# Norm passes of caches and late weights issued only in the units of branch A

## The chip, the cores and the metric

The kernel runs on one core of a Trainium2 chip. The metric is the device time of one launch in microseconds (us). The core has five engines with a queue each: TensorE (PE, with its weight loads as PEld), VectorE (DVE), ScalarE (ACT), GpSimd (POOL) and SyncE (SP). In this kernel SP issues every DMA, so that all loads, stores and DMA transposes stand in one queue, in the order in which the program was built.

## What is computed

The reference is one layer of a streaming encoder: 2048 prompt rows and 128 sample rows (8 streams of 16) of width 1024. Cut to what matters here:

```
h  = rms_norm(x, norm_g) * (1 + scale) + shift          # scale, shift, gate from c @ w_ada + b_ada
qa, ka, va, za, qb, kb, vb, zb, ga, gb = split(h @ w_in)
A: 4 heads, two score maps each, chunk-causal:  w = softmax(s1) - lam * softmax(s2);  oa = w @ va
B: 8 heads, stick-breaking:  a = sigmoid(z) * prod over later keys of (1 - sigmoid(z));  ob = a @ vb
ya = (rms_norm(oa) * silu(za)) @ w_branch_a;   yb = (ob * silu(zb)) @ w_branch_b
y  = rms_norm(x + gate * ((sigmoid(ga) * ya + sigmoid(gb) * yb) @ w_out), final_g)
```

The sample rows attend to caches of 512 earlier keys and values (cache_a_k, cache_a_v, cache_b_k, cache_b_v) as well. All rotated keys and values are outputs too.

## The kernel before

**Numbers.** Products of f32 operands are made of two f16 halves each, three matmuls for one. To split an operand, the kernel needs a bound on its size: the sum of its squares. For the weights and caches that are used late (w_branch_a, w_branch_b, w_out and the four caches) these sums come from 80 *norm passes*, here called spares: `norms()` at L801 makes a list of them. Each takes the next of a ring of staging buffers (`free`), loads 128 x 1024 f32 into it (512 KB, SP, L811) and squares and sums it on ACT (L255). Nothing reads their sums before `early_work` (L1153) and the last stage.

**Stages.** First (L875 to L1084) the conditioning, the norms and the transposed f16 halves of h, which go to DRAM (hT_d). Then the attention loop (L1171 to L1198), and last the output stage with the sample rows' attention (L1203 on).

**Units.** The attention loop goes over 8 units u and in each over 17 tiles: the sample tile NT, and the row tiles t = 0 to 15. Even units are one head of branch A, odd units two heads of branch B; below they are called A0, B1, A2, B3, A4, B5, A6, B7. In each step the loop issues scores of tile t (L597; matmuls L611, L612), the product with the values for the tile two steps back (L663 for B, L659 to L661 for A), and projections for a tile some five steps ahead (L409; gate columns L476). The work of a tile grows with t, since the attention is causal.

**What each engine does.** In an A tile DVE evicts the scores (L530), ACT takes exponentials (L119), DVE combines the two maps (L575) and splits them with ACT. In a B tile ACT takes two sigmoids (L119), DVE runs the product as a scan (L588), POOL multiplies (L594), ACT casts (L544) and DVE subtracts (L545). In both, SP then issues a DMA transpose of the weights (wt, L552) for PE. SP also loads h for the projections (hg, L386, three buffers), and stores keys, values and z (L457 to L460), gates (L480) and outputs (L653).

**Preparing weights.** When a unit starts, `prepare_unit` (L290) puts the pieces for the next unit's projection weights into the list `back`: loads into ring buffers (L305, and L307 for the gate columns), their Squares, and cuts into f16 halves (L273, L275, L278), in which DVE, ACT and POOL read the loaded buffer. The loop issues one or two of these in each step until `back` is empty, which it is from tile 9 on in units 0 to 6. In unit 7 nothing is prepared. When a unit's projection starts, five tiles before its scores, the buffers of the unit before it return to the ring. Before that the ring holds few buffers: 6 in A0, 4 in the middle units, 2 in A6, because the last unit's gate weights are twice as wide.

**Where spares are issued.** In a step with an empty `back` the loop issues spares: the length of the list, divided by a count of steps that are left, rounded up.

**Order.** The order in which Python issues the work is only a priority. The framework's scheduler decides the order on each engine: it lifts an instruction ahead of others once its buffers are free, loads on SP above all. The order is then fixed in the program.

**After the spares.** `early_work` starts when the projections and the spares are all issued.

Of the kernel before, what the change touches and what calls it, by code (L numbers as in the profile page):

```python
# [32 lines left out]
NT = SEQ // P  # L33
# [57 lines left out]
def interleave(*streams):  # L91

    order = []
    for i, pieces in enumerate(streams):
        lo, hi = 0.0, 1.0
        if isinstance(pieces, tuple):
            pieces, lo, hi = pieces
        total = sum(cost for cost, _ in pieces) or 1.0  # L100
        done = 0.0
        for j, (cost, fn) in enumerate(pieces):
            order.append((lo + (hi - lo) * (done + cost / 2) / total, i, j, fn))
            done += cost
    for _, _, _, fn in sorted(order, key=lambda e: e[:3]):
        fn()
# [3 lines left out]
def layer_kernel(ctx: ExitStack, tc: tile.TileContext, a: dict):  # L110
# [486 lines left out]
    def scores(U, t, jobs):  # L597

        sc, kind = U["sc"], U["kind"]
        nch = t // 4 + 1  # L600
        own = [new_job(U, t, c, t + 1) for c in range(1 + kind)]
        jobs += own

        def chunk(c, ch):
            job = own[c if kind == 1 else 0]
            seg = job["segs"][ch * 4 // SEG]
            n = 512 if ch < t // 4 else (t % 4 + 1) * P
            p = bank("s")
            qst, kk = U["q", t], U["k"][ch]
            diag = ch == t // 4  # L610
            T.matmul(p[:, 0:n], qst[:, c, :], kk[:, c, 0:n], start=True, stop=False)  # L611
            T.matmul(p[:, 0:n], qst[:, 2 + c, :], kk[:, c, 0:n], start=False, stop=not diag)  # L612
            if diag:
                m = mask_a if kind == 0 else mask_b
                T.matmul(p[:, n - m.shape[1] : n], idb, m, start=False, stop=True)
            evacuate(job, seg, c, p, ch * 512 - seg["lo"] * P, n, sc[:, 3:4], sc[:, 4:5], ch)
            if kind == 0:
                if diag and c == 1:
                    softmax_pair(job)
                return  # L620
            i = job["segs"].index(seg)
            later = job["segs"][i + 1] if i + 1 < len(job["segs"]) else None
            stick(seg, later, ch * 512 - seg["lo"] * P, n, p)
            if ch * 4 == seg["lo"]:
                if later is not None:
                    stick_weights(job, later, None)
                if i == 0:
                    stick_weights(job, seg, later)

        order = [(c, ch) for ch in range(nch) for c in range(2)] if kind == 0 else \  # L630
                [(c, ch) for c in range(2) for ch in reversed(range(nch))]
        return [(2.0 if ch < t // 4 else (t % 4 + 1) / 2, lambda c=c, ch=ch: chunk(c, ch)) for c, ch in order]
# [33 lines left out]
    def pv(job):  # L666

        U, t, c = job["U"], job["t"], job["c"]
        segs = job["segs"] if U["kind"] == 0 else job["segs"][::-1]
        order = [(seg, j) for seg in segs for j in range(seg["hi"] - seg["lo"])]  # L670

        def block(i):
            seg, j = order[i]
            if i == 0 and (U["kind"] == 0 or c == 0):
                U["po", t] = bank("o")
            pv_block(job, seg, U["po", t], j, U["v"][seg["lo"] + j], i == 0, i == len(order) - 1)
            if i == len(order) - 1 and (U["kind"] == 0 or c == 1):
                store(U, t, natural(U, t, U.pop(("po", t))))

        return [(1.5, lambda i=i: block(i)) for i in range(len(order))]  # L680
# [120 lines left out]
    def norms():  # L801

        srcs = [w[:, k, :] for w in (w_ba, w_bb) for k in range(4)] + [w_out[:, k, :] for k in range(KT)]
        srcs = [(src, wsums[:, i : i + 1]) for i, src in enumerate(srcs)]
        srcs += [(caches[name][:, i * 8 : i * 8 + 8, h * P : (h + 1) * P], csums[:, cache_column(name, h), i : i + 1])
                 for name in caches for h in range(4) for i in range(4)]

        def one(src, dst):
            st = free.pop(0)
            free.append(st)  # L810
            load(out=st if len(src.shape) == 2 else st.rearrange("p (j n) -> p j n", n=P), in_=src)  # L811
            sum_squares(st, 1024, dst)

        return [lambda src=src, dst=dst: one(src, dst) for src, dst in srcs]
# [3 lines left out]
    spare = norms()  # L818
# [36 lines left out]
    def position(x):  # L855

        m = min(int(x), len(steps) - 1)
        return starts[m] + (starts[m + 1] - starts[m]) * (x - m)

    def take(target, need):  # L860

        i = at[0]
        out = []
        while i < len(line) and (i < target or any(m <= need for m, _ in line[i : i + 14])):
            out.append((1.0, line[i][1]))
            i += 1
        at[0] = i
        return out

    def duration(t):  # L870
        return SAMPLE_TIME if t == NT else TILE_TIME + (t + 1) / 4
# [281 lines left out]
    def early_work():  # L1153


        res = ctx.enter_context(tc.tile_pool(name="resw", bufs=1, side="right", reuse_waits="tile"))
        L["wb"] = res.tile([P, 2, 2, 4, D], F16, name="wb")
        L["inp"] = ctx.enter_context(tc.tile_pool(name="inp", bufs=1, side="right", reuse_waits="tile"))
        L["s"] = [scales(total(add_up(wsums[:, lo : lo + 8], 8)), con, f"s_w{lo}") for lo in (0, 8)]
        stage = cutting.enter_context(tc.tile_pool(name="stage", bufs=1, side="right", reuse_waits="tile"))  # L1160

        def first(t):
            if "orms" not in L:
                L["orms"] = rsqrt(osums[:, 0:NT, :].rearrange("p t h -> p (t h)"), 4 * NT, P, con, "orms")
            states[t] = inputs(t)

        made = [lambda k=k, j=j, br=br: cut(L["wb"][:, br, :, :, :], (w_ba, w_bb)[br], k, j, L["s"][0], br + k, stage, "wst2", 1)
                for br in range(2) for k in (0, 2) for j in range(2)]
        return made + [lambda t=t: first(t) for t in tiles[0:2]]

    for n in range(len(steps) + PV_LAG):  # L1171
        made, qk, vs = [], [], []
        if n < len(steps):
            u, t = steps[n]
            past += duration(t)
            if t == NT and u < 7:
                back += prepare_unit(u + 1)
            if back:
                for fn in back[: -(-len(back) // max(1, W_READY - t % NT))]:
                    back.pop(0)()  # L1180
            else:
                for _ in spare[: -(-len(spare) // ((NT + 1 - t % NT) + 8 * (6 - min(u, 6))))]:
                    spare.pop(0)()
            if t < NT:
                qk = scores(units[u], t, made)
        if n >= PV_LAG:
            for job in jobs[n - PV_LAG]:
                vs += pv(job)
        target = position(len(steps) * past / whole + LEAD)
        pieces = take(target, min(n + 1, len(steps) - 1))  # L1190
        if at[0] == len(line) and not pieces and not spare:
            if cuts is None:
                proj.close()
                cuts = early_work()
            pieces = [(1.0, fn) for fn in cuts[: -(-len(cuts) // (len(steps) + PV_LAG - n))]]
            del cuts[: len(pieces)]
        interleave(pieces, qk, (vs, V_LO, V_HI))
        jobs.append(made)  # L1198
# [149 lines left out]
```

## Time and profile before

| | us |
|---|---|
| three runs | 2440.4, 2433.63, 2436.15 |
| their median | 2436.15 |
| the profiled execution | 2436.39 |
| its span (first to last instruction) | 2434.6 |

Mean granted clock of PE over the span: 0.949. In rows of the profile an instruction is named by its engine, its line in the kernel before, its operation and its tiles (out<-in), without buffer numbers: `wa` and `wb` are the ring's buffers. A wait row says who waited for whom, then us in all, the number of times and the longest. SPq is SP's queue. In a timeline row the first number is the start, the second the length, and what stands in brackets is the engine's idle time before it and what ended it.

### The profile page before, as it was taken

How to read it: one execution, taken by the hardware profiler on the slowest of the kernel's cores; microseconds unless marked ns; L12 is line 12 of the kernel's file. 1: busy time of each engine (PE TensorE's matmuls, PEld its weight loads, DVE VectorE, ACT ScalarE, POOL GpSimd, SP SyncE). 2: the span in 40 equal slices, each digit the busy share in tenths (PEclk: the TensorE clock that was granted, in tenths of full speed). 3: DMA queues.
4: the chain of work that ended last, by engine and by line, in shares of the span. 5: the costliest groups of instructions: out<-in, count | busy, mean ns of one | idle time of the engine just before them, and what ended most of it. 6: DMA issues, size and time to landing. Idle time of an engine off the chain costs nothing. (4 is left out here: it accounts for less than half of the span.)

```text
span 2434.6 us, 45193 instructions
## 1 busy us (share of the span) xinstructions
PE 2138.5 (88%) x16366; PEld 1252.6 (51%) x16366; DVE 1811.3 (74%) x3769; ACT 1601.5 (66%) x3200; POOL 840.5 (35%) x671
## 2 busy tenths in 40 slices
PE   4879998998999898899889889999974888989897
PEld 2445655565665455566555556555542344444443
DVE  4878787886667788667678975656787888887765
ACT  3758888886768887666778866656775544454552
POOL 1833033452202245310234631002354554445422
PEclk7979999999999999999999999999977889889999
DMA  9669869985876998577689756756679988888521
GB/s 328 218 207 228 195 158 233 216 177 136 208 198 158 222 196 179 133 169 184 158 191 194 161 139 166 158 126 138 142 168 239 276 226 238 221 232 225 163 101 53
DMA packets 854000, 453.98 MB, mean 186 GB/s; under 512 B 538922, under 2 KB 806362, under 8 KB 853264
## 3 DMA queue, kind: packets, MB, share of 16 engines
q1 hardware_dynamic: 853776, 451.09, 74.3%
q8 instruction: 128, 2.10, 0.4%
q14 instruction: 96, 0.79, 0.1%
HBM read 249.87 MB, written 73.44 MB: 133 GB/s over the span
## 5 line engine op out<-in xcount | busy, mean ns | idle before, releaser
L594 POOL TENSOR_TENSOR sc_p<-sc_p,sc_n 128x127 f32<-128x127 f32 (+7 forms) x192 | 320.0, 1669 | 765.4 <-DVE sc_n L588 734.4
L409 PEld LDWEIGHTS <-hg 128*128 128x128 f16 x3120 | 276.1, 99 | 312.4 <-DMA hg<-hT_d 61.0
L409 PE MATMUL ps_mm<-wa,hg 128*128 128x512 f16 x1590 | 400.3, 384 | 30.2 <-DMA hg<-hT_d 30.1
L409 PE MATMUL ps_mm<-wb,hg 128*128 128x512 f16 x1530 | 388.7, 383 | 19.1 <-DMA hg<-hT_d 19.1
L476 PEld LDWEIGHTS <-hg 128*128 128x128 f16 x2856 | 276.0, 98 | 92.8 <-DVE qst L504 4.3
L588 DVE TENSOR_TENSOR_SCAN sc_n<-ps_s,sc_n,zero_t 128x512 f32<-128x512 f32 x192 | 245.6, 1279 | 56.9 <-ACT ps_s L119 51.0
L611 PE MATMUL ps_s<-k,qst 128*128 128x512 f16 (+3 forms) x640 | 226.4, 355 | 36.3 <-DVE sc_n L588 32.2
L545 DVE TENSOR_TENSOR sc_n<-sc_p,sc_n 128x128 f16<-128x128 f32 (+7 forms) x192 | 227.7, 1191 | 27.7 <-ACT sc_n L544 27.3
L476 PE MATMUL ps_t<-wb,hg 128*128 128x256 f16 (+1 forms) x1734 | 244.5, 293 | 0.7 <-DVE qst L504 0.6
L119 ACT ACTIVATE sc_p<-ps_s,usc 128x512 f32<-128x512 f32 (+3 forms) x320 | 205.8, 643 | 46.5 <-PE ps_s L612 29.6
L612 PE MATMUL ps_s<-k,qst 128*128 128x512 f16 (+3 forms) x640 | 226.4, 355 | 0.0
L1235 PE MATMUL ps_mm<-wb,uT 128*128 128x512 f16 x816 | 199.8, 396 | 16.9 <-DVE o L1134 9.2
L119 ACT ACTIVATE ps_s<-ps_s,usc 128x512 f32<-128x512 f32 (+3 forms) x328 | 201.1, 613 | 0.0
L663 PE MATMUL ps_o<-v,wt 128*128 128x128 f16 x1088 | 161.2, 226 | 43.2 <-DMA wt<-sc_n 42.9
L1274 PE MATMUL ps_o<-wo,yT 128*128 128x512 f16 x816 | 193.4, 392 | 5.5 <-POOL wo L275 2.6
L442 POOL TENSOR_TENSOR rot<-pr,rope 128x256 f32<-128x256 f32 x68 | 61.9, 910 | 381.8 <-ACT pr L423 312.4
L544 ACT CAST sc_n<-sc_p 128x128 f16<-128x128 f32 (+7 forms) x192 | 155.1, 814 | 54.8 <-POOL sc_p L594 54.1
L530 DVE TENSOR_SCALAR_CACHE_REDUCE sc_p<-ps_s,usc 128x512 f32<-128x512 f32 (+3 forms) x160 | 106.6, 666 | 75.7 <-PE ps_s L612 54.8
L663 PEld LDWEIGHTS <-wt 128*128 128x128 f16 x1088 | 104.8, 102 | 98.3 <-DMA wt<-sc_n 54.1
L476 PE MATMUL ps_t<-wa,hg 128*128 128x256 f16 (+1 forms) x1122 | 148.4, 282 | 1.0 <-DVE qst L504 1.0
L664 PE MATMUL ps_o<-v,wt 128*128 128x64 f16 x1088 | 148.5, 198 | 0.0
L530 DVE TENSOR_SCALAR_CACHE_REDUCE sc_n<-ps_s,usc 128x512 f32<-128x512 f32 (+3 forms) x160 | 106.6, 666 | 48.9 <-PE ps_s L612 25.7
(317 smaller groups left out, 4566.0 us busy)
## 6 DMA issues: line engine op xcount, KB each, us to landing
hg<-hT_d SPq DMA_DIRECT2D x130, 512.0 KB, 4.6
g<-g_d SPq DMA_DIRECT2D x34, 512.0 KB, 7.1
out_dram<-pr SPq DMA_DIRECT2D x204, 64.0 KB, 1.9
g_d<-gt SPq DMA_DIRECT2D x102, 128.0 KB, 3.7
wide<-in_w_ada_dram SPq DMA_DIRECT2D x12, 1024.0 KB, 9.1
wa<-in_w_in_dram SPq DMA_DIRECT2D x34, 256.0 KB, 6.2
z_d<-pr SPq DMA_DIRECT2D x136, 64.0 KB, 1.8
o_d<-o SPq DMA_DIRECT2D x136, 64.0 KB, 2.9
```

What stands on the lines that cost most here:

```text
L119: i = S.activation(**kw)
L409: T.matmul(box["p"], box["h"][:, hi, k, :], U["w"][k][:, wi, :], start=(n == 0), stop=(n == 3 * KT - 1))
L476: T.matmul(box["g"][:, 0:gw], box["h"][:, hi, k, :], U["wg"][k // per][:, k % per, wi, :], start=(j == 0), stop=(j == 3 * KT - 1))
L530: V.tensor_scalar(out=dst[:, lo : lo + n], in0=p[:, 0:n], scalar1=sc_pos, scalar2=None, op0=ALU.mult, op1=ALU.max, accum_out=job["mx"][:, ...
L545: V.tensor_tensor(out=lo, in0=src, in1=hi, op=ALU.subtract)
L588: V.tensor_tensor_scan(out=dst[:, lo : lo + n][:, ::-1], data0=src[:, 0:n][:, ::-1], data1=zero_t[:, 0:1].to_broadcast([P, n]), initial=fi ...
L594: G.tensor_tensor(out=p[:, 0:m], in0=p[:, 0:m], in1=n[:, 1 : m + 1], op=ALU.mult)
L611: T.matmul(p[:, 0:n], qst[:, c, :], kk[:, c, 0:n], start=True, stop=False)
L612: T.matmul(p[:, 0:n], qst[:, 2 + c, :], kk[:, c, 0:n], start=False, stop=not diag)
L663: T.matmul(po[:, c * P : (c + 1) * P], wt[:, wj, :], vt[:, c, :, :], start=first, stop=False)
L1235: T.matmul(pb, st["u"][:, ui * 8 + br * 4 + k, :], wb[:, br, wi, k, c], start=(n == 0), stop=(n == 11))
L1274: T.matmul(po, st["y"][:, yi * 8 + k, :], wo[:, wi, k, c], start=(n == 0), stop=(n == 3 * KT - 1))
```

## The change

Spares are issued in even units alone (branch A), with another divisor: the steps left in this unit, plus four for each unit that is left before unit 6. In unit 6 the divisor is the number of tiles that are left, so that the list is empty after its last tile. The whole diff:

```diff
@@ -1178,8 +1178,9 @@
             if back:
                 for fn in back[: -(-len(back) // max(1, W_READY - t % NT))]:
                     back.pop(0)()
-            else:
-                for _ in spare[: -(-len(spare) // ((NT + 1 - t % NT) + 8 * (6 - min(u, 6))))]:
+            elif u % 2 == 0:
+
+                for _ in spare[: -(-len(spare) // ((NT - t % NT) + 4 * (6 - u)))]:
                     spare.pop(0)()
             if t < NT:
                 qk = scores(units[u], t, made)
```

`-(-a // b)` is a / b rounded up; W_READY is 9 and NT is 16. The list of spares and their order in it stay as they are, so that another spare falls on a given step, and the ring hands its buffers to other loads from there on.

## The prediction

> **What bounds the kernel now.** I read the page first, then busy time by unit (stretches), then PE's and SP's waits, then the timelines of two stalls.
>
> ```profile
> span 2434.6 us, 45193 instructions
> PE 2138.5 (88%) x16366; PEld 1252.6 (51%) x16366; DVE 1811.3 (74%) x3769; ACT 1601.5 (66%) x3200; POOL 840.5 (35%) x671
> ```
>
> PE is the busiest engine, but the stages differ. I cut the trace where the score matmuls (L611) of a unit's tile 0 begin; tile t has 2*(t//4+1) of them, so they can be counted off in order. B1 (the first unit of branch B), B3, B5, then A2, A4, A6; columns: stretch, length, busy us (instructions) of PE, weight loads, DVE, ACT, POOL, then granted clock, DMA share, GB/s:
>
> ```profile
> 306.00:528.00 222.00, 200.47 (x1660) 126.70 (x1659) 180.56 (x274) 186.96 (x376) 96.27 (x68) 0.98 0.89 200
> 735.00:963.00 228.00, 203.16 (x1654) 127.31 (x1652) 185.20 (x274) 186.37 (x372) 97.61 (x68) 0.98 0.85 192
> 1170.00:1398.00 228.00, 200.90 (x1653) 127.41 (x1652) 191.96 (x275) 181.92 (x363) 99.71 (x68) 0.99 0.81 179
> 528.00:735.00 207.00, 194.16 (x1526) 123.90 (x1523) 133.63 (x373) 139.80 (x314) 34.57 (x41) 0.99 0.72 176
> 963.00:1170.00 207.00, 195.04 (x1530) 124.45 (x1529) 134.68 (x373) 133.74 (x303) 34.20 (x42) 0.99 0.65 161
> 1398.00:1617.00 219.00, 204.29 (x1512) 123.69 (x1510) 137.96 (x382) 139.26 (x310) 37.33 (x42) 0.98 0.62 147
> ```
>
> In A, PE is busy some 94% and ACT 65%; in B, PE 89%, ACT and DVE 82%: B has less room for extra ACT work, which is the change's argument. Where B loses PE time is its first half (tiles 0 to 8); A's second half (tiles 9 to 15) is all but full:
>
> ```profile
> 735.00:834.00 99.00, 85.71 (x670) 53.04 (x668) 74.10 (x134) 80.07 (x171) 29.37 (x24) 0.97 0.78 190
> 834.00:963.00 129.00, 117.45 (x985) 74.27 (x984) 111.10 (x141) 106.30 (x201) 68.24 (x44) 0.99 0.90 193
> 618.00:735.00 117.00, 113.61 (x926) 75.10 (x925) 76.84 (x204) 83.48 (x180) 13.03 (x15) 1.00 0.80 192
> 1055.00:1170.00 115.00, 113.76 (x927) 75.20 (x926) 76.30 (x201) 76.77 (x168) 12.58 (x15) 1.00 0.68 169
> ```
>
> PE's waits in those stretches: two rows of B3's first half (735 to 834), then the longest of the second halves of A2, A4 and A6 (columns: us in all, times, longest):
>
> ```profile
> PE ps_o L663 <- DMA wt<-sc_n: 6.5, 6, 2.0
> PE ps_mm L409 <- DMA hg<-hT_d: 6.1, 4, 3.0
> PE ps_o L659 <- DMA wt<-sc_n: 3.1, 2, 1.9
> PE ps_mm L409 <- DMA hg<-hT_d: 0.7, 1, 0.7
> PE ps_mm L409 <- DMA hg<-hT_d: 3.4, 3, 1.9
> ```
>
> PE waits for DMAs that come late out of SP's one queue, rather than for ACT.
>
> **The change, part by part.** *What moves.* A spare is one 512 KB load on SP (L811) and one Square on ACT (L255). By the rule at L1178 to 1183, with `back` empty in tiles 9 to 15 only (in unit 7 throughout), the units 0 to 7 take 14, 14, 14, 13, 8, 8, 8, 1 spares now and 21, 0, 21, 0, 21, 0, 17, 0 after: 35 leave the B units, and 36 come to the A units (one from unit 7). The list is empty before unit 7's tile 0 either way, so early_work starts when it did. In ACT time:
>
> ```profile
> L255 ACT ACTIVATE junk<-wa x68: 1039/1057/1103, 83.3 to 1607.8; 128x1024 f16<-128x1024 f32 x68
> L255 ACT ACTIVATION_READ_ACCUMULATOR junk<-wa x68: 185/187/248, 84.3 to 1608.8; 128x1 f32 x68
> ```
>
> 1.057 + 0.187 = 1.24 us each, 35 x 1.24 = 43 us of ACT moved from B to A. Nothing is added or removed; what counts is which wait each one lengthens.
>
> *Where the spares really stand.* The built program doesn't issue them in tiles 9 to 15 of B: the scheduler lifts loads to where a buffer comes free. B3's first half holds all 13:
>
> ```profile
> L811 SPq DMA_DIRECT2D wb<-in_cache_b_k_dram x7: 368/433/1069, 809.5 to 832.5; - x7
> ...
> L811 SPq DMA_DIRECT2D wb<-in_cache_a_v_dram x6: 383/387/470, 760.8 to 797.0; - x6
> ```
>
> There they stall PE in two ways. First, head of line (SP's timeline, PE's, and the clock):
>
> ```profile
> 789.25 0.44 SPq L460 DMA_DIRECT2D z_d<-pr  x1
> 794.31 0.39 SPq L811 DMA_DIRECT2D wb<-in_cache_a_v_dram  x1
> 794.79 0.55 SPq L386 DMA_DIRECT2D hg<-hT_d  x1
> 799.65 3.66 PE L409 MATMUL ps_mm<-wb,hg 128*128 128x512 f16 x10 [3.03 <-DMA hg<-hT_d]
> 799.00:802.40 3.40, 2.75 (x7) 1.04 (x8) 3.29 (x5) 1.81 (x5) 1.62 (x1) 0.50 1.19 293
> ```
>
> SP stands 4.6 us before a spare's load, whose buffer DVE still reads for a weight cut; the hg load behind it lands late and PE idles 3.03 us. Then the granted clock is 0.50 for 3.4 us, which costs 1.7 us more. The Trainium skill (TensorE: Matmul & The Clock Gate, "Part 1: The HAM clock gate") says that the clock halves after an idle window of about 3.4 us; here 3.03 us of idling was enough, so the row decides.
>
> Second, bursts: seven spares within 23 us hold SP, and the transposes behind them start late (two rows of SP's timeline, then three of PE's).
>
> ```profile
> 809.50 0.43 SPq L811 DMA_DIRECT2D wb<-in_cache_b_k_dram  x1
> ...
> 821.93 5.13 SPq L552 DMA_TRANSPOSE wt<-sc_n  x2
> 815.52 2.76 PE L409 MATMUL ps_mm<-wb,hg 128*128 128x512 f16 x12 [1.91 <-DMA hg<-hT_d]
> ...
> 826.65 0.23 PE L663 MATMUL ps_o<-v,wt 128*128 128x128 f16 x1 [1.95 <-DMA wt<-sc_n]
> ...
> 829.29 0.23 PE L663 MATMUL ps_o<-v,wt 128*128 128x128 f16 x1 [1.36 <-DMA wt<-sc_n]
> ```
>
> *What B gains.* In the changed kernel's built order the first stall does not go. With no spare in the way, the four weight loads of the unit after next (L305) rise from B's second half into its first, into the same buffers, and wait for the same DVE cuts: in B1 and B5 hg stands right behind such a load, in B3 behind it and four more issues. Gain 0; loss at about 0.4 us an issue some 1.5 us over B3 and B5 (bounds 0 and 4). The bursts do go: 1.91 + 1.95 + 1.36 = 5.2 us in B3. I take half as PE's gain, since DVE and ACT of that half (75 and 81% busy) are late next, and the same in B1 and B5: -7.8 (bounds 0 and -16). B's second half loses the Squares of those weights, 4 in each unit, and the last of the spares'. But PE waits there for DVE's scan, and DVE (86%) stays: I take -1 a unit, -3 in all (bounds -9 and +7, the upper end from the port rival below). B: -7.8 - 3 + 1.5 = -9.3.
>
> *What A loses.* A2 (14 spares) and A4 (8) last the same 207 us: 0 for each spare. Their second halves are 117 and 115 us: 2/6 = 0.33 us each. If the Square delayed PE in full it would be 1.24. I take 0.17, the middle of the two that are measured: 36 x 0.17 = +6.1. A6 is its own case: only two free buffers until unit 7's projection returns unit 6's, so SP waits for a Square in front of a load, with hg loads behind it:
>
> ```profile
> SPq L811 <- ACT junk L255: 6.1, 2, 3.6
> ```
>
> PE already loses 3.4 us to hg there with 8 spares, and 17 come; in the built order two or three now stand ahead of most hg loads. I add +4 (bounds 0 and +10). A: +10.1 (bounds 0, and 36 x 0.33 + 10 = +22).
>
> *Elsewhere* the built order differs too, through B7 and the output stage. No row prices it; by the 5 us by which two units of equal work with nearly equal spares differ (B1 222, B3 228), I allow 5 us either way and take 0.
>
> **Sum**: -9.3 + 10.1 = +0.8. The profiled execution took 2436.39 us (span 2434.6 and 1.8 around it), 0.2 above the median of 2436.15. Forecast: 2437 us, no change. About 0.3%, 7.3 us, is what a measurement of this kernel can tell.
>
> **The rivals.** *(a) Faster: SP is what holds B.* For it: PE's longest waits are for hg and wt, and they stand beside the bursts. Against: B1 with 14 spares lasts 222 us and B5 with 8 lasts 228, so fewer spares have not meant a shorter unit. Price: the burst stalls go in full, -16; B's second half gives -9 as ACT falls back; A costs only 5: -20, 2416. It decides if B's first halves fall below 95 us.
>
> *(b) Slower: SP's queue in A takes over.* Three spares a tile instead of one or two, over two to four buffers; each load waits for the Square of the one two to four before it, and hg and the transposes queue behind. PE has no slack in A's second half, so each such wait is paid. Price: A +22, two half-clock spells at 1.7, B -9: +16, 2452. It decides when hg and wt waits in A's second halves exceed some 17 us over four units, against 3.1 + 0.7 + 3.4 = 7.2 in the rows above.
>
> *(c) Slower: B speeds ACT into a contended port.* DVE's subtraction in B's second half, in B1, B3, B5:
>
> ```profile
> L545 DVE TENSOR_TENSOR sc_n<-sc_p,sc_n 128x1024 f16<-128x1024 f32 (+7 forms) x29 | 34.7, 1203 | 3.2 <-ACT sc_n L544 3.1
> L545 DVE TENSOR_TENSOR sc_n<-sc_p,sc_n 128x1024 f16<-128x1024 f32 (+7 forms) x29 | 39.2, 1360 | 2.3 <-ACT sc_n L544 2.3
> L545 DVE TENSOR_TENSOR sc_n<-sc_p,sc_n 128x1024 f16<-128x1024 f32 (+7 forms) x28 | 42.8, 1534 | 3.8 <-ACT sc_n L544 3.7
> ```
>
> It grows from 1203 to 1534 ns as a unit's spares fall from 14 to 8: the less ACT lags, the more this falls on POOL's multiply (L594). If B1 and B3 go to B5's level and all three by as much again, that is 8.1 + 3.6 + 3 x 8 = 36 us of DVE, of which I let half reach the end while the bursts give 8 back: +10, with A +10: +20, 2456. It decides if L545 passes 1.6 us. The Trainium skill (SBUF — State Buffer, "Who interferes with whom") has the rule: a DVE operation with two SBUF inputs and a GpSimd one that reads SBUF exclude each other, and the later blocks. The three rows agree, but they don't say which engine pays.
>
> *(d) The change does nothing to the order*: excluded, the built order moves the spares on SP and ACT as the counts say.
>
> **How the numbers follow.** Forecast 0.38, faster (a) 0.29, slower (b) 0.21 and (c) 0.12, together 0.33. The forecast's own range is 2436 - 7 to 2436 + 7, 2429 to 2443. The range for 8 in 10 reaches to the cases' times, 2416 to 2456, with 2 more above because (b)'s bounds are not met by any row: 2416 to 2458.
>
> **What would show it.** Right: no L811 between 306 and 528; SP goes straight from L480 to the transposes around B's tile 7, and the wt wait of 1.95 us there is gone; the hg stall of about 3 us one tile earlier is still there, behind an L305; B units 218 to 226 us, A2 and A4 208 to 212, A6 220 to 226. Wrong: A's second halves with no more than 8 us of hg and wt waits in all and B below 216 (then a); hg waits of over 17 us in A (then b); L545 over 1.6 us (then c); or units as predicted and a difference of over 6 us after unit 7, which I have no term for.

## The result and the profile after

The kernel after takes 2443.21 us, median of 20 runs (2438.39 to 2454.52), against 2436.95 for the kernel before in 20 runs beside them (2429.14 to 2443.2). The ratio is 1.0029, 95% interval 1.0018 to 1.0039: slower by some 7 us, just inside the 0.3% that the prediction counted as no change. The forecast was 2437, with 2429 to 2443 as its own range and 2416 to 2458 for 8 in 10: the median stands at the upper end of the first (0.2 past it) and well inside the second.

The page of the kernel after, its first lines. The busy sums hardly differ from those of before; in 2437.3 us a redistribution shows only by stretch.

```profile
span 2437.3 us, 45250 instructions
...
PE 2150.6 (88%) x16366; PEld 1259.8 (52%) x16366; DVE 1802.5 (74%) x3769; ACT 1601.9 (66%) x3200; POOL 838.9 (34%) x671
```

Its units B1, A2, B3, A4, B5, A6, cut and with columns as in the prediction:

```profile
313.00:528.00 215.00, 201.47 (x1689) 129.55 (x1688) 183.11 (x274) 173.40 (x347) 98.98 (x68) 0.99 0.79 172
528.00:743.00 215.00, 197.92 (x1501) 123.83 (x1498) 134.07 (x373) 145.89 (x329) 35.14 (x42) 0.96 0.78 184
743.00:965.00 222.00, 203.69 (x1682) 130.72 (x1680) 182.86 (x275) 173.78 (x346) 96.22 (x68) 0.98 0.77 169
965.00:1174.00 209.00, 194.32 (x1504) 122.29 (x1503) 135.26 (x374) 146.28 (x330) 35.44 (x42) 0.98 0.79 190
1174.00:1393.00 219.00, 202.09 (x1688) 130.13 (x1687) 182.80 (x275) 173.59 (x346) 95.98 (x68) 0.98 0.75 171
1393.00:1624.00 231.00, 211.12 (x1529) 124.71 (x1526) 141.27 (x384) 148.59 (x327) 39.13 (x41) 0.98 0.63 158
```

The change did what it was meant to do: B1, B3 and B5 are shorter by 7, 6 and 9 us, and their DMA share fell from 0.81-0.89 to 0.75-0.79. A2, A4 and A6 are longer by 7, 2 and 12, and the share of A2 rose from 0.72 to 0.78, that of A4 from 0.65 to 0.79. To a tenth of a us, by the starts of each unit's first score matmul, with six experiments that are told below:

| unit, us | A0 | B1 | A2 | B3 | A4 | B5 | A6 | B7 starts at |
|---|---|---|---|---|---|---|---|---|
| before | 170.9 | 221.6 | 207.6 | 227.9 | 206.9 | 228.2 | 218.4 | 1616.8 |
| after | 177.4 | 214.7 | 215.1 | 222.2 | 208.5 | 219.1 | 230.9 | 1623.5 |
| no spares at all | 170.0 | 217.0 | 204.5 | 215.7 | 199.7 | 217.0 | 214.5 | 1574.6 |
| before without B's 36 spares | 170.4 | 218.1 | 207.4 | 215.9 | 203.2 | 219.5 | 220.3 | 1590.6 |
| after, thin Squares | 178.2 | 216.1 | 218.4 | 215.3 | 217.8 | 219.9 | 226.2 | 1628.7 |
| after, loads on ACT's queue | 175.4 | 215.3 | 209.7 | 223.1 | 206.6 | 221.3 | 229.7 | 1617.4 |
| after, small loads | 174.0 | 214.3 | 214.3 | 220.8 | 212.4 | 220.3 | 218.5 | 1611.7 |
| after, no spares in A6 | 182.3 | 216.8 | 218.5 | 215.7 | 212.7 | 216.4 | 218.2 | 1617.8 |

From before to after the three B units give 21.7 us and the four A units take 28.1. B7 starts 6.7 us later; in the two profiled executions 4 of that come back behind it.

These times are of one execution of each kernel, and not all from one session: `before` and `after` were profiled where before's median was 2436.95, the experiments where it was 2442 to 2444, so a unit of an experiment reads some 0.6 us longer for that alone. The execution without spares (2392.61) is 10.4 us below its kernel's median, that of `after` 4.0 below.

Where A loses: A6's second half (tiles 9 to 15) before, the second halves of A0, A2, A4 and A6 after, then PE's waits in these four.

```profile
1490.00:1617.00 127.00, 122.42 (x892) 72.72 (x890) 77.67 (x208) 81.02 (x178) 11.63 (x15) 1.00 0.64 150
```

```profile
205.00:313.00 108.00, 98.44 (x757) 59.90 (x755) 74.90 (x206) 91.08 (x199) 10.36 (x14) 0.98 0.93 230
620.00:743.00 123.00, 114.57 (x901) 73.42 (x899) 76.67 (x201) 88.42 (x193) 12.68 (x15) 0.97 0.89 208
1052.00:1174.00 122.00, 113.95 (x898) 73.10 (x896) 76.45 (x200) 88.53 (x192) 11.98 (x15) 0.97 0.87 208
1480.00:1624.00 144.00, 132.51 (x917) 76.10 (x916) 81.66 (x210) 90.71 (x195) 14.28 (x15) 0.96 0.64 163
```

```profile
PE ps_o L659 <- DMA wt<-sc_n: 9.6, 4, 3.9
...
PE ps_mm L409 <- DMA hg<-hT_d: 6.3, 3, 4.5
PE ps_o L659 <- DMA wt<-sc_n: 2.2, 3, 1.4
...
PE ps_mm L409 <- DMA hg<-hT_d: 7.0, 4, 4.3
PE ps_o L659 <- DMA wt<-sc_n: 1.0, 2, 0.5
...
PE ps_mm L409 <- DMA hg<-hT_d: 8.2, 3, 5.4
PE ps_o L659 <- DMA wt<-sc_n: 1.1, 2, 0.9
```

PE's work in A2's second half is the same (113.6 us before, 114.6 now), but 117 us became 123: the hg and wt waits there are 8.5 us now. Over the four halves they are 35.4 us; counted in the same way they were 10.6 before.

The waits are 24.8 us more, but the four halves grew by 36.3 (the table of second halves further down). The clock has a part in the rest: before, it was 1.00 in all four, with no wait over 2.0 us; after, it is 0.98, 0.97, 0.97 and 0.96, with a longest wait of 3.9 to 5.4 us in each. Each half's length times what its clock lacks of 1.00 is some 15 us in all, an estimate from these rows; a part of it falls into the waits themselves. So a long wait can be paid for twice.

How such a wait comes about, on the longest one of A2: SP's timeline, then PE's, then the stretch around it.

```profile
641.70 1.04 SPq L811 DMA_DIRECT2D wb<-in_cache_a_v_dram  x1
642.84 6.43 SPq L552 DMA_TRANSPOSE wt<-sc_n  x2
649.36 1.41 SPq L458 DMA_DIRECT2D out_dram<-pr  x1
...
652.24 0.43 SPq L811 DMA_DIRECT2D wa<-in_cache_a_v_dram  x1
...
653.87 0.41 SPq L386 DMA_DIRECT2D hg<-hT_d  x1
...
655.90 5.84 SPq L552 DMA_TRANSPOSE wt<-sc_n  x2
```

```profile
659.92 1.46 PE L409 MATMUL ps_mm<-wa,hg 128*128 128x512 f16 x3 [4.45 <-DMA hg<-hT_d]
```

```profile
655.00:664.00 9.00, 4.55 (x14) 1.59 (x12) 2.66 (x9) 4.78 (x11) 0.00 (x0) 0.72 0.99 206
```

A spare's load is issued at 641.70. The two transposes behind it take 6.43 us to issue; SP then has no pause up to the hg load at 653.87, which lands some 6 us later (PE starts on it at 659.92), while the DMA engines are 0.99 busy. PE idles 4.45 us and the granted clock of that stretch is 0.72. Transposes that begin between 2 us before a spare's load and 6 us after it take 2.67 us to issue in the A units (mean of 33), the others 1.84 (61). The spare's load itself takes only 0.4 to 1 us of SP's time. What stretches is the transpose beside it. How much of A's loss comes of that stretching is a question for the experiments.

### The profile page after: what moved, and what is told of

It reads as the page before. It is cut to its first block, busy times and chain, and to the rows that moved or that the text cites. A ratio compares the mean times of both kernels' runs of the same rounds, so it can differ in the third digit from the quotient of the medians.

```text
span 2437.3 us, 45250 instructions
## 1 busy us (share of the span) xinstructions
PE 2150.6 (88%) x16366; PEld 1259.8 (52%) x16366; DVE 1802.5 (74%) x3769; ACT 1601.9 (66%) x3200; POOL 838.9 (34%) x671
## 3 DMA queue, kind: packets, MB, share of 16 engines
q1 hardware_dynamic: 853776, 451.09, 74.6%
## 5 line engine op out<-in xcount | busy, mean ns | idle before, releaser
L594 POOL TENSOR_TENSOR sc_p<-sc_p,sc_n 128x127 f32<-128x127 f32 (+7 forms) x192 | 312.7, 1633 | 765.0 <-DVE sc_n L588 740.4
L409 PE MATMUL ps_mm<-wb,hg 128*128 128x512 f16 x2142 | 544.9, 386 | 28.4 <-DMA hg<-hT_d 26.3
L476 PE MATMUL ps_t<-wa,hg 128*128 128x256 f16 (+1 forms) x1938 | 271.3, 291 | 0.0
L409 PE MATMUL ps_mm<-wa,hg 128*128 128x512 f16 x978 | 253.7, 391 | 19.0 <-DMA hg<-hT_d 19.0
L545 DVE TENSOR_TENSOR sc_n<-sc_p,sc_n 128x128 f16<-128x128 f32 (+7 forms) x192 | 220.1, 1151 | 35.5 <-ACT sc_n L544 35.3
L1236 PE MATMUL ps_mm<-wb,uT 128*128 128x512 f16 x816 | 208.8, 409 | 20.0 <-DVE o L1134 11.1
L663 PE MATMUL ps_o<-v,wt 128*128 128x128 f16 x1088 | 166.8, 226 | 45.1 <-DMA wt<-sc_n 44.8
L664 PE MATMUL ps_o<-v,wt 128*128 128x64 f16 x1088 | 154.0, 199 | 0.0
L1236 PEld LDWEIGHTS <-uT 128*128 128x128 f16 x816 | 83.1, 104 | 127.0 <-issue 52.4
```

The source lines that it names most:

```text
L409: T.matmul(box["p"], box["h"][:, hi, k, :], U["w"][k][:, wi, :], start=(n == 0), stop=(n == 3 * KT - 1))
L476: T.matmul(box["g"][:, 0:gw], box["h"][:, hi, k, :], U["wg"][k // per][:, k % per, wi, :], start=(j == 0), stop=(j == 3 * KT - 1))
L545: V.tensor_tensor(out=lo, in0=src, in1=hi, op=ALU.subtract)
L594: G.tensor_tensor(out=p[:, 0:m], in0=p[:, 0:m], in1=n[:, 1 : m + 1], op=ALU.mult)
L663: T.matmul(po[:, c * P : (c + 1) * P], wt[:, wj, :], vt[:, c, :, :], start=first, stop=False)
L1236: T.matmul(pb, st["u"][:, ui * 8 + br * 4 + k, :], wb[:, br, wi, k, c], start=(n == 0), stop=(n == 11))
```

## The experiments

The kernel before took 2442 to 2444 us in the three sessions of the experiments, so ratios to the kernel before in the same session are compared, not times. The theory at the start was that spares cost PE time only where SP's queue makes hg or wt late; the rivals were the ACT time of the Squares, the bytes on the DMA engines, and the chance of the built order.

**No spares at all.**

```diff
-    spare = norms()
+    spare = []
+    V.memset(wsums, 1000.0)
+    V.memset(csums, 1000.0)
```

> The kernel after without the 80 norm passes (their loads and Squares are left out, the sums are constants). It prices all of them together. Theory (a spare costs PE time only where it makes hg or wt come late, some 28 us in A after, 16 to 22 us in B before): about 2405 to 2420, A0 163 to 166, A2 and A4 200 to 205, A6 208 to 214, B units as after (213 to 222). Rival (what an A unit lost is the ACT time of the Squares, 1.24 us each): A0 145 to 150, A2 190, A6 210, in all about 2345 to 2370. Rival (the units differ by the chance of the built order, not by the spares): A units stay within 4 us of the kernel after, about 2440.

Measured: 2402.97 us, ratio 0.9836 (0.9812 to 0.986). All 80 cost the kernel after 0.9836 to 1.0029, 1.9% or 47 us. PE's hg and wt waits of A's second halves are 1.5 us. The rows are the second halves of A2, A4 and A6:

```profile
611.00:728.00 117.00, 115.47 (x939) 76.27 (x937) 77.46 (x206) 72.52 (x161) 13.18 (x15) 1.00 0.57 140
1028.00:1143.00 115.00, 115.00 (x934) 76.02 (x933) 77.24 (x203) 71.92 (x160) 13.18 (x15) 1.00 0.59 142
1448.00:1575.00 127.00, 127.00 (x916) 74.94 (x914) 78.85 (x208) 73.11 (x159) 11.99 (x15) 1.00 0.54 125
```

PE is busy nearly all the time there at a clock of 1.00, with DMA engines at 0.54 to 0.59: room for some loads, until they come too dense. The theory's B units came out as expected; the time fell just below its 2405 to 2420, A0 missed by most (170.0 for 163 to 166), A4 and A6 by 0.5 us or less. It also shows that A4 is by itself 4.8 us shorter than A2 (199.7 and 204.5), which the prediction could not see.

**B's relief alone**: before, with the spares that fall into B units left out. They are 36, the 35 of B1, B3 and B5 and the single one of B7, which the expectation counted among those that stay (in the built order of before its load stands in A6). Two added lines, left out here, set the sums to a constant.

```diff
                 for _ in spare[: -(-len(spare) // ((NT + 1 - t % NT) + 8 * (6 - min(u, 6))))]:
-                    spare.pop(0)()
+                    fn = spare.pop(0)
+                    if u % 2 == 0:
+                        fn()
```

> The kernel before with the 35 norm passes that fall into B units left out (their sums are constants), the 45 others where they were: the part of the change that relieves B, alone. Theory (B's units and A's add up): B1, B3 and B5 at 214 to 219 as without any, a gain of some 20 to 28 us, A0, A2, A4 and A6 within 4 us each of before (171, 207, 207, 218): 0.988 to 0.992 of before. Rival (what B gains is not from its own norm passes, or is given back in the next A unit): over 0.995.

Measured: 2408.7 us, ratio 0.9854 (0.9835 to 0.9874), more than expected: 36 spares in B cost 1.46%, 36 us, 1.0 each by the medians; in the traces the three B units are 24.2 us shorter, 0.7 for each of their 35. The A units are within 4 us of before, so the parts add up. Putting the 36 into A instead costs 0.9854 to 1.0029, 1.75% or 43 us, 1.2 each. And 0.9836 against 0.9854: the first 44 in A cost next to nothing by the medians (4 us, the intervals overlap). By the starts of B7 in the two traces (1574.6 and 1590.6) it would be 16 us, but some 10 of these are the profiled execution without spares, which was that much below its median. So the price in A is not one price: it is low for the first and high for those that come on top.

**The mirror: all 80 in B.**

```diff
-            elif u % 2 == 0:
-                for _ in spare[: -(-len(spare) // ((NT - t % NT) + 4 * (6 - u)))]:
+            elif u % 2 == 1:
+                for _ in spare[: -(-len(spare) // ((NT - t % NT) + 4 * (5 - min(u, 5))))]:
```

> The mirror of the change: norm passes only in B1, B3 and B5 (28, 28, 24). Against the kernel without them, those of before cost some 0.8 us each in B (28 us for 35) and 0.3 in A (15 us for 45); after, 0.54 each in A. If the place has its price: B's 80 cost 64 us, 2460 to 2475, B units 230 or more, A units as without norm passes (170, 204, 200, 214). If only the number counts and not the place: 2435 to 2447.

Measured: 2487.45 us, ratio 1.0179 (1.0158 to 1.0199); B1, B3 and B5 last 245, 251 and 237 us. That is above the 2460 to 2475 expected, and A2, A4 and A6, in which no spare stands, last 210.5, 207.7 and 217.9, some 3 to 8 us more than without any. All in A is better than all in B by 1.5%: the idea of the change is sound, only its comparison was not with all in B, but with a spread over both.

**Is it ACT's time?** Each Square over 128 columns in place of 1024.

```diff
-            sum_squares(st, 1024, dst)
+            sum_squares(st, P, dst, P)
```

> The kernel after with each norm pass's Square over 128 of the 1024 columns (so the sums cover an eighth); its load stays whole. ACT loses some 0.9 us for each of 80, and a buffer comes free by as much earlier. Theory (SP's queue and the DMAs): 2435 to 2443, hg waits in A's second halves still 25 to 35 us, with a gain in A6 only, where SP waits for the Square. Rival (ACT time of the Squares): A0, A2 and A6 fall by 10 us or more in all, 2410 to 2425.

Measured: 2445.86 us, ratio 1.0006 (0.9985 to 1.0027) against 1.0029: at most a few us. The hg and wt waits of A's second halves are 37.8 us, as many as after. A6 fell (231 to 226), but A2 rose by 3 and A4 by 9. ACT's time as the main cause falls. A4's rise is a warning too: with 21 spares in each of after, thin Squares, ACT's queue and small loads it lasts 208.5, 217.8, 206.6 and 212.4 us, so some us in a single unit are no price by themselves.

**Is it SP's queue?** The loads on ACT's queue.

```diff
-            load(out=st if len(src.shape) == 2 else ...
+            nc.scalar.dma_start(out=st if len(src.shape) == 2 else ...
```

> The kernel after, with the loads of the norm passes issued on ACT's queue: the same bytes and the same kind of queue as SP's, but none of them stands in SP's. A load waits there mostly for ACT's own Square of the buffer, which is over by then. Theory 1 (SP's queue): 2415 to 2428. Theory 2 (bytes): 2436 to 2448, with transposes still slow to issue. Third way (ACT stands still where a buffer is still read by DVE's cuts, with the exponentials behind it): 2450 or more, in A's second halves, with ACT waits at the load's line.

Measured: 2442.15 us, ratio 1.0 (0.9984 to 1.0016): 0.3% better than after, and the waits are still there, 34.0 us in A's second halves. No spare stands in SP's queue now; its timeline and PE's at A6's longest stall:

```profile
1522.20 0.34 SPq L457 DMA_DIRECT2D out_dram<-rot  x1
1524.03 7.46 SPq L552 DMA_TRANSPOSE wt<-sc_n  x2
```

```profile
1535.63 0.29 PE L659 MATMUL ps_o<-v,wt 128*128 128x128 f16 x1 [5.67 <-DMA wt<-sc_n]
```

SP is idle when the transposes come, and they take 7.46 us all the same. So a spare in SP's own queue isn't what makes the transposes slow, and the waits are as many without it. The Trainium skill (DMA: Bandwidth & Descriptors, "Issuing engines are not separate DMA queues") says that DMAs from different issuing engines run on the same 16 DMA engines and that another issuer saves sequencer time only; the trace agrees, with 34.0 us of waits against 35.4.

That is not to say that SP's queue costs nothing. The four A units are 10.5 us shorter together than after, and their second halves 16.7: in A2 and A4 no wait is over 1.8 us, where the longest were 4.5 and 4.3, and the clock stays at 1.00. The stretch from B7's start on is 12.3 us longer (826.1), though no spare stands in it; no run shows why, and so the 0.3% is not SP's price alone.

**The same on GpSimd's queue**, once in the kernel after and once in the kernel before (`nc.gpsimd.dma_start`).

> The kernel after, with the loads of the norm passes issued on GpSimd's queue in place of SP's; bytes, Squares and their place are those of after. Theory (SP's queue is what they cost): the hg and wt waits of A's second halves fall from 35 us to under 15, A falls by 15 to 28, B stays as after: 2415 to 2428, faster than both. Rival (ACT time or the DMAs' bytes are the cost): A stays, 2438 to 2448, and the hg waits are still there. A third way: POOL's multiply of B is not touched, as no spare stands in a B unit, so a loss in B would speak against the theory.

> The kernel before with the same edit: the loads of the norm passes on GpSimd's queue. Theory (in B it is SP that the spares hold): B1, B3 and B5 fall by the 5 to 9 us that they gained after, A by 0 to 3 us each: 2410 to 2420, and the change would then be worth nothing or a loss. Rival (B's gain after was ACT's, 35 Squares less): B units stay at 222 to 228, 2430 to 2440. Rival (POOL's sequencer waits for a buffer in front of B's multiply L594): slower, B 230 or more, 2450.

Measured: 2482.14 us, ratio 1.0165 (1.0141 to 1.0188), and 2492.32 us, 1.0225 (1.0198 to 1.0252): the theories' times were missed by far, and the queue made it worse. The B units lengthen in both (by 15 us together in the first, in which no spare stands in them); of the readings only the third of the second run has the direction, with 2450 and B units of 230 or more (254, 236 and 233). The waits of A's second halves rise to 66.5 us in the first, and in the second B1 rises to 254 us. The transposes in 262 to 300 us of the first (columns: count, ns at least, median, at most), and its DMA queues (packets, MB):

```profile
L552 SPq DMA_TRANSPOSE wt<-sc_n x4: 1851/4888/10872, 267.1 to 287.7; - x4
```

```profile
q1 hardware_dynamic: 784912, 409.15, 67.8%
q0 software_dynamic: 11520, 41.95, 6.3%
```

A spare goes as 11520 / 80 = 144 packets of 3.6 KB here; on SP's queue it was 861 of 0.6 KB, as the count of q1 fell from 853776 by 68864. Beside these few large packets a transpose takes up to 10.87 us. The Trainium skill (DMA: Bandwidth & Descriptors, "Queues, rings and completion order") says that each DMA engine takes turns between queues packet by packet; a queue with six times larger packets would then get a larger share beside the transposes, if what the profile counts as packets is what the page calls so. The rows fit, but no run here varies the packet size alone: GpSimd's way of issuing changed with it.

**Is it the bytes?** Loads of 64 KB, Squares of the whole buffer, once in the kernel after and once in the mirror.

```diff
-            load(out=st if len(src.shape) == 2 else st.rearrange("p (j n) -> p j n", n=P), in_=src)
+            load(out=st[:, :P], in_=src[:, :P] if len(src.shape) == 2 else src[:, 0, :])
```

> The kernel after, but each norm pass loads 64 KB in place of 512 KB and squares the whole buffer (seven eighths of each sum are of what the buffer held before). SP issues as many loads, ACT does as much; the bytes are an eighth. After the first four runs ACT time is out, and the kernel without norm passes, 2403, is the floor. Theory 1 (SP's queue: issues, and what stands behind them): 2433 to 2443, hg and wt waits in A's second halves still 25 us or more. Theory 2 (bytes on the DMA engines, which make the transposes and hg land late): 2405 to 2420, and those waits fall to 15 us or less.

> The mirror (norm passes in B1, B3 and B5 only, 28, 28, 24), with loads of 64 KB in place of 512 KB and Squares of the whole buffer (seven eighths of each sum are of what the buffer held before). With whole loads it took 1.018 of before. Theory (B's price is that of the bytes, on DMA engines that are busy 0.8 to 0.9 there): 0.985 to 0.995, transposes issued beside a norm pass no slower than others. Rival (SP that stands before a load whose buffer DVE still reads, and ACT's time in a half where ACT is 82% busy): 1.008 or more.

Measured: 2431.62 us, ratio 0.9957 (0.9939 to 0.9974), and 2444.74 us, 1.0003 (0.9987 to 1.0018). Both lie between the two theories. In the kernel after seven eighths of the bytes are 0.7% of the 1.9% that the spares cost, and 15 of the 35 us of waits; in the mirror 1.8% of 3.4%. Transposes beside a spare are no slower than others any more (1.82 us against 1.96 in A; in the B units of the mirror 1.99 against 1.97, where it was 4.12 against 1.92 with whole loads). They were in B1's second half of the mirror, first with whole loads, then with 64 KB, then without any spares:

```profile
L552 SPq DMA_TRANSPOSE wt<-sc_n x29: 1192/2366/7574, 404.2 to 550.0; - x29
```

```profile
L552 SPq DMA_TRANSPOSE wt<-sc_n x29: 1189/1865/5231, 408.7 to 548.9; - x29
```

```profile
L552 SPq DMA_TRANSPOSE wt<-sc_n x28: 1192/1962/4191, 403.1 to 521.2; - x28
```

So the slow transposes are the bytes' doing, and seven eighths of the bytes are 37% of the price in A and 51% in B.

But that the slow transposes are what costs the time is not shown. Of the 12.7 us that the A units gain with small loads, A6 has 12.4; A2's second half stays at 122 us and A4's at 121, with fast transposes beside the spares and waits of 7.0 and 6.0 us in place of 8.4 and 8.0. In the mirror B3 gives 21 us and B5 8, but B1 only 2 (245.2 to 242.8), though its transposes are as fast as without spares. The rest stays with small loads, and no single edit removes it: less ACT time and another queue gave 0.2 and 0.3%. In the kernel with small loads the longest waits left in A's second halves are 2.2 us for wt, part of them behind the unit's own weight loads (L305), which the scheduler placed elsewhere: two transposes beside these loads take 5.06 us to issue. How much of the rest is order and how much the sum of ACT and SP wasn't told apart.

**Is A6's ring the price?** No spares in A6; 28, 28 and 24 in A0, A2 and A4.

```diff
-                for _ in spare[: -(-len(spare) // ((NT - t % NT) + 4 * (6 - u)))]:
+                for _ in spare[: -(-len(spare) // ((NT - t % NT) + 4 * (4 - min(u, 4))))]:
```

> The kernel after with the norm passes in A0, A2 and A4 only (28, 28, 24), none in A6 with its ring of two buffers. A6 lost 16 us to its 17 norm passes (230.9 against 214.5 without any), the others 7, 11 and 9 to 21 each. If the small ring is A6's price: A6 falls by 14 to 17, the others rise by 0.45 a spare, 8 in all: 2432 to 2438. If a norm pass costs alike everywhere, or if more a tile make each dearer: 2440 to 2455.

Measured: 2429.03 us, ratio 0.9942 (0.9924 to 0.9959): faster than before, and by 0.9% than after. A6 lasts 218.2 us, 12.7 less (14 to 17 were expected); A0, A2 and A4 rise to 182.3, 218.5 and 212.7, 12.5 together (8 were expected). The end of A6 as it is there, from late in its tile 8:

```profile
1485.00:1618.00 133.00, 133.00 (x980) 79.20 (x979) 80.88 (x217) 77.81 (x171) 12.00 (x15) 1.00 0.53 125
```

Against 1480 to 1624 after: PE without an idle moment, clock 1.00 in place of 0.96. B7 starts 6 us earlier than after and, in the profiled executions, 5 more are gained behind it; the medians say 21. The remaining 10 are no gap: 6.8 are the difference of the two sessions (before took 2436.95 and 2443.78), 3.3 the place of the two profiled executions below their medians (4.0 and 0.7).

What these units say is not what the run was made for. The four A units take 731.7 us together, and 731.9 after: the 17 spares cost A0, A2 and A4 what they had cost A6. What got shorter is B3 and B5 (222.2 to 215.7 and 219.1 to 216.4, B1 2.1 longer), in which no spare stands either way, and the stretch behind B7's start. That this is the built order is likely, but was not tried. Nor is A6's ring the price by itself: with small loads the same two buffers serve the same 17 spares, SP stands 6.1 us in front of them for a Square in A6's second half (7.7 after), and A6 lasts 218.5 us.

**A6's spares to B7 instead** (21, 21, 21 in A0, A2, A4, and 17 in B7).

```diff
-            elif u % 2 == 0:
-                for _ in spare[: -(-len(spare) // ((NT - t % NT) + 4 * (6 - u)))]:
+            elif u in (0, 2, 4, 7):
+                for _ in spare[: -(-len(spare) // (max(1, 10 - t % NT) if u == 7 else (NT - t % NT) + 7 * (4 - u) // 2 + 7))]:
```

> The kernel after with A6's 17 norm passes moved to the last unit, B7, in which no weights are prepared and the ring is full (21, 21, 21 and 17 in A0, A2, A4 and B7). Theory (A6's price is its ring of two buffers and the bytes): A6 falls from 231 to 218 or less, B7 rises by 17 times 0.3 to 0.5, 5 to 8 us: 0.992 to 0.997 of before. Rival (in B7, where PE is all but full in the first half, they cost 0.8 to 1 each as in other B units, or the weights' cuts of the output stage start late): 0.999 to 1.005.

Measured: 2437.22 us, ratio 0.9972 (0.996 to 0.9984). A6 falls from 231 to 220, the time from B7 on rises by 7 in the trace. B7's rise is as the theory had it; A6 missed its 218 by 2, and the ratio lies just above 0.992 to 0.997 and below the rival's 0.999. B7 is no free place either.

**The two edits that helped, together**: no spares in A6, loads on ACT's queue.

> The norm passes in A0, A2 and A4 only (28, 28, 24), their loads on ACT's queue: the two edits that helped, together. If they add: 0.989 to 0.993 of before, against 0.994 with SP's queue. If the loads' bytes are what is left, ACT's queue brings nothing here: 0.993 to 0.997.

Measured: 2453.0 us, ratio 1.0035 (1.0017 to 1.0052), and neither reading holds: ACT's queue costs 0.9% here. A0, A2 and A4 rise by another 8, 8 and 10 us (in an execution 11 us above its kernel's median). At 28 spares a unit the issue itself holds ACT's sequencer (8 issues around A2, then PE's waits in A0):

```profile
L811 ACTq DMA_DIRECT2D wb<-in_cache_a_v_dram x8: 374/928/4452, 625.3 to 683.9; - x8
```

```profile
PE ps_o L659 <- DMA wt<-sc_n: 15.6, 6, 8.3
PE ps_mm L409 <- DMA hg<-hT_d: 7.0, 1, 7.0
```

An issue that takes 0.37 us at the least takes up to 4.45, and ACT does nothing for 5.4 us around that one. How much of the 0.9% that is, and how much the density, wasn't told apart.

## Why the prediction was right, and where it was not

The time came out as forecast because two terms that were each less than half of what happened cancelled: B -9.3 was -21.7, A +10.1 was +28.1, the sum +0.8 was +6.4 at the unit level and +6.3 in the medians. The mechanism named for B was found; of A's, the waits for hg and wt were, but not all that lengthened A. That the two errors cancelled is luck: the bounds of A (+22) did not hold what A lost. Of its ranges for the units, B3, B5 and A4 came out inside, B1, A2 and A6 outside. The sizes failed in these steps.

- *B: "I take half as PE's gain, since DVE and ACT of that half are late next."* The bursts' gain came in full. PE's three waits for hg and wt late in each first half were 4.9, 5.2 and 5.8 us before (B1, B3, B5); after, none over 0.9 us is left there. B's first halves went from 300.0 us together to 283.9, -16.1, which is the lower bound that was given, and PE's hg and wt waits in them from 42.5 to 26.3; without any spares the halves are 275.9. What DVE and ACT took back was little. B's second halves gave -5.6 (nearly all in B3) against -3. The run without B's spares says the same of the three units: -24.2, against -21.7 after.
- *"The first stall does not go"*: right. PE's stall for hg is 2.39 us in B1 (2.63 before) and 3.47 in B5 (2.86). In B3 it changed its kind: SP stands 4.61 us in front of a weight load of the unit after next, and PE waits; SP's timeline of B3 and PE's:

```profile
764.53 0.33 SPq L386 DMA_DIRECT2D hg<-hT_d  x1
769.47 2.35 SPq L305 DMA_DIRECT2D wa<-in_w_in_dram  x3
771.92 1.22 SPq L552 DMA_TRANSPOSE wt<-sc_n  x1
```

```profile
775.63 0.29 PE L663 MATMUL ps_o<-v,wt 128*128 128x128 f16 x1 [4.97 <-DMA wt<-sc_n]
```

  There it strikes a transpose and not hg, in tile 3 and not 6, and costs 4.97 us and not some 3: B3's first half gained only 0.5 us, where B1's and B5's gained 6.8 and 8.8. The wt wait of 1.95 us around tile 7 is gone, as foretold.
- *A: "A2 (14 spares) and A4 (8) last the same 207 us: 0 for each spare"*, and 0.33 each from the second halves. This is the step that failed. The two units are not of equal work: without spares A2 is 4.8 us longer than A4, and its second half 1.5. Compared with themselves, and with the number of spares whose loads are issued in the half itself (the scheduler puts the rest of a unit's into its first half):

| second half, us (spares) | A0 | A2 | A4 | A6 |
|---|---|---|---|---|
| none | 100.3 (0) | 115.1 (0) | 113.6 (0) | 126.5 (0) |
| before | 102.7 (8) | 116.7 (8) | 114.5 (2) | 126.5 (6) |
| after | 109.4 (15) | 122.3 (14) | 121.9 (14) | 143.1 (14) |
| ACT's queue | 103.7 (14) | 118.6 (14) | 118.3 (14) | 139.4 (14) |
| small loads | 107.8 (15) | 122.2 (14) | 120.8 (14) | 128.8 (14) |
| none in A6 | 115.3 (22) | 128.4 (20) | 123.0 (16) | 126.4 (0) |

  The 24 of before cost 4.9 us, 0.2 each; the 33 on top cost 36.3, 1.1 each. The 0.17 was the price of a spare that falls into slack, and it was carried on to those that no longer did. It also had no term for the clock, which no second half of before had lost. A's first halves gave 8.2 of it back (A4's 92.4 to 86.6, A6's 92.0 to 87.8), which the prediction had no term for.
- *A6 +4*, with 1.5 for its nine more spares: it was +12.5, at the upper end of its bounds (10 and 9 x 0.33), and A in all passed the bound of +22. What was told is there: SP stands in front of a load until a Square is done, with hg loads behind. That this standing is the price is not shown: at the longest stall SP does not stand, the hg load is issued behind two spares at 1532.57 and PE starts on it at 1540.33, and with small loads the standing stays while the price goes.

```profile
SPq L811 <- ACT junk L255: 7.7, 4, 3.6
```

```profile
1531.47 0.39 SPq L811 DMA_DIRECT2D wb<-in_cache_b_v_dram  x1
1531.94 0.53 SPq L811 DMA_DIRECT2D wa<-in_cache_b_v_dram  x1
1532.57 0.86 SPq L386 DMA_DIRECT2D hg<-hT_d  x1
```

```profile
1540.33 1.89 PE L409 MATMUL ps_mm<-wb,hg 128*128 128x512 f16 x4 [5.38 <-DMA hg<-hT_d]
```

  14 loads there cost 16.6 us in the second half, where 14 in A2 cost 7.2; with small loads 2.3 and 7.1.
- *Rivals (a) and (b)* were held to exclude each other. Both happened: two of three B first halves fell below 95 us (90.8, 98.4, 94.7), and hg and wt waits in A's second halves are 35.4 us against a threshold of 17. What was put down to SP's queue in both was in part the bytes of the loads: in B3's burst the seven loads took SP 0.43 us each by the median, the two transposes behind them 5.13 us.
- *Rival (c)* fell. L545 in the second halves of B1, B3 and B5 after:

```profile
L545 DVE TENSOR_TENSOR sc_n<-sc_p,sc_n 128x1024 f16<-128x1024 f32 (+7 forms) x30 | 41.6, 1391 | 5.0 <-ACT sc_n L544 5.0
L545 DVE TENSOR_TENSOR sc_n<-sc_p,sc_n 128x1024 f16<-128x1024 f32 (+7 forms) x30 | 41.8, 1399 | 5.0 <-ACT sc_n L544 5.0
L545 DVE TENSOR_TENSOR sc_n<-sc_p,sc_n 128x1024 f16<-128x1024 f32 (+7 forms) x30 | 42.1, 1410 | 4.9 <-ACT sc_n L544 4.9
```

  Without spares all three are at 1.4 us: B1 rose to it from 1.2, but B5 fell to it from 1.53, and 1.6 was not reached. The trend over B1, B3 and B5 was three points, not a law.
- *Elsewhere 0*: B7 and the output stage took 4 us less in the profiled execution. That this part varies with the built order is likely (807 to 826 us over the kernels here) but was not tried; and as the profiled execution of after was 4.0 us below its median, the 4 us may be no more than that. The 5 us allowed for it were to be the difference of B1 and B3, which is 6 by the rows (222 and 228).

## What to carry to other kernels

The price of background loads isn't a constant for each. In A's second halves the first 24 cost PE 0.2 us each and the 33 on top 1.1 each, so a price read at the present density must not be carried to a higher one. Two units can stand for two doses of the same thing only if their times without it are known to be equal. Where PE waits for long, count its clock as well as the wait: here 24.8 us more of waits came with halves that are 36.3 us longer. And when a place is left out because it looks dear, compare the sum over all places: without spares in A6 the kernel was 0.9942 of before, but the four A units took as long as with them.

## What was not expected of the hardware

- A DMA transpose's issue on SP takes longer beside a 512 KB load: 2.67 us on average (33 of them) against 1.84 in the A units of after, 4.12 (33) against 1.92 in the B units of the mirror, and no longer beside a 64 KB one (1.99 against 1.97). It doesn't matter whether SP or ACT issued the load (2.54 against 1.86 with ACT's queue). Single ones take 4.4 to 5.3 us without any spare too, and up to 10.9 with loads from GpSimd's queue in packets of 3.6 KB.
- Issuing a load from ACT isn't free: 0.37 us mostly, up to 4.45 us where the DMA engines are full (a DMA share of 1.00 over 70 us around it).
- PE's clock doesn't follow from the longest wait alone: it stayed at 1.00 over A0's second half with ACT's queue, where one wait was 3.73 us, and fell to 0.98 over A0's with small loads, where none was over 2.24.
